# Transposing a normalised row tile one PSUM bank at a time, with every other bank read by VectorE

## The chip, the cores and the metric

One core of a Trainium2 chip runs the whole program. The metric is the device time of one execution in microseconds (us); the kernel before takes 2774.78 us, the median of 3 runs (2773.95 to 2774.79).

## The reference, cut to what matters

One layer of a hybrid decoder is computed for 1024 prompt rows and 64 sample rows (1088 rows of 1024 values, float32). What matters here stands between the mixer and the feed-forward part:

```python
def decoder_layer(x, ...):
    mix, new_win, hg_state = token_mixer(rms_norm(x, norm_mix_pre), ...)   # ends in merged @ w_out
    x = x + rms_norm(mix, norm_mix_post)
    f, conv_buf = conv_ffn(rms_norm(x, norm_ffn_pre), conv_buf0, w_ffn_a, w_ffn_b, ffn_conv_w, ffn_conv_b, w_ffn_d)
    x = x + rms_norm(f, norm_ffn_post)
```

So for each row: the product with `w_out`, a norm, the addition of `x`, a second norm with the gains `norm_ffn_pre`, and then the feed-forward products, which need the normalised rows transposed (features on the partitions).

## The kernel before, in words

The kernel has three phases. Phases 1 and 2 (projections, attention, recurrence, memory attention, gates) are not touched. Phase 3 (`phase3`, from L1386) goes through the 1088 rows in nine row tiles: tiles 0 to 7 of 128 rows, and tile 8 of the 64 sample rows. They are taken in the order 0 and 2 together, then 1, 3, 4, 6, 5, 7, 8. For each tile there are three steps.

- `sums` (L1418): the product with `w_out`, 48 matmuls of 512 columns (8 blocks, 2 halves, 3 products of high and low parts) into two PSUM banks (L1428). The banks come from three pools of two: `ps_u` (tiles 0, 3, 5), `ps_n` (2, 4, 8) and `ps_d` (1, 6, 7). So tile 4 must have read its sums before the matmuls of tile 8 can start.
- `norms` (L1433): `x` is loaded (L1438, on the queue of SyncE, in order), the sums are squared on ScalarE (L1442), the factor is found by `rstd` (L160 to L165, tiny operations that go between VectorE and ScalarE), the sums are scaled (L1447) and `x` is added (L1448) on VectorE, the result is stored by a DMA of GpSimd (L1449), squared on ScalarE (L1451), a second `rstd`, and the rows are scaled on ScalarE (L1453) into `pn_x`. `pn_x` and `pn_y` have two buffers each, so the load of `x` for a tile waits until the transposes of the tile two before it have read their `pn_x`.
- The transposes, at the end of `norms`: eight chunks of 128 x 128 are transposed on TensorE (L1458), four into each of two PSUM banks `ps_t`, and each chunk is copied on ScalarE with its gain (L1461) into `R`. There are only those two `ps_t` banks, and the framework keeps two engines from touching one bank of one tile at the same time: a transpose into a bank waits for the copy of the chunk before it in that bank. With two banks, two transposes can be under way, one for each bank, and then their two copies.

From pairs of tiles, `combos` (L1531) makes on ScalarE and VectorE the sums and splits that the first feed-forward products read: columns 0 to 511 (called t = 0) need tiles 0 to 3, columns 512 to 1087 (t = 1) tiles 4 to 8. `prep_a` with `side_a` (L1565 to L1598) loads and splits the feed-forward weights, in SBUF that held `w_out` (its load, L1578, waits for the last matmul on it). `up` (L1606) does the products, 84 matmuls for each t (L1627). The last three kinds of product of t = 0 need PSUM banks that `ps_n` and `ps_t` held, so they wait for the last copy of the last tile and for the small state that is transposed after it (L1502, copied at L1504). Two blocks of `combos` and the weights are traced under `behind`, which makes the scheduler place them after a given instruction.

Each engine and each DMA queue runs its instructions in an order fixed when the kernel is built, by a list scheduler with a model of the times; at run time an instruction that waits holds up all behind it on its engine.

Of the kernel before, what the change touches and what calls it, by code (L numbers as in the profile page):

```python
# [21 lines left out]
AF = mybir.ActivationFunctionType  # L22
ALU = mybir.AluOpType
AX = mybir.AxisListType

P = 128
# [33 lines left out]
VR_BIN, VR_FFN, VR_HGN, VR_LB = 0, 80, 88, 89  # L60
# [59 lines left out]
class Builder:  # L120
# [1265 lines left out]
    def phase3(self, early):  # L1386

        tc, nc, I, O = self.tc, self.nc, self.I, self.O
        PS = bass.MemoryType.PSUM
        with ExitStack() as es:  # L1390
# [42 lines left out]
            def norms(i, ps, R, half):  # L1433

                a, e = ROWT[i]
                rows = e - a
                x = xp.tile([P, D], F32, name="pn_x")[:rows]
                nc.sync.dma_start(x, self.xrows(a, e))  # L1438
                y = xp.tile([P, D], F32, name="pn_y")[:rows]
                ss = self.sm.tile([P, 2], F32, name="pn_ss")[:rows]  # L1440
                for u in range(2):
                    nc.scalar.activation(y[:, :512], ps[u], AF.Square, accum_out=ss[:, u:u + 1])  # L1442
                nc.vector.tensor_add(ss[:, 0:1], ss[:, 0:1], ss[:, 1:2])
                r = self.rstd(ss[:, 0:1], rows, D)
                for u in range(2):
                    v = slice(u * 512, (u + 1) * 512)
                    nc.vector.scalar_tensor_tensor(y[:, v], ps[u], r, gb[:rows, v], op0=ALU.mult, op1=ALU.mult)  # L1447
                    nc.vector.tensor_add(y[:, v], y[:, v], x[:, v])  # L1448
                nc.gpsimd.dma_start(self.x1d[a:e], y)  # L1449
                s2 = self.sm.tile([P, 1], F32, name="nrm_ss")[:rows]  # L1450
                nc.scalar.activation(x, y, AF.Square, accum_out=s2)  # L1451
                r = self.rstd(s2, rows, D)
                nc.scalar.activation(x, y, AF.Copy, scale=r)  # L1453
                for c in range(8):
                    if c % 4 == 0:
                        pt = self.next_bank()
                    p = pt[:, c % 4 * P:c % 4 * P + rows]
                    nc.tensor.transpose(p, x[:, c * P:(c + 1) * P], self.ident[:rows, :rows])  # L1458
                    g = self.vec[:, VR_FFN + c:VR_FFN + c + 1]
                    dst, src = (R[:, c], p.rearrange("p (h n) -> p h n", h=2)) if half is None else (R[:, c, half], p)  # L1460
                    nc.scalar.activation(dst, src, AF.Copy, scale=g)  # L1461
            new_R = lambda w=P: self.rp.tile([P, 8, 2, w], F32, name=f"R{w}", bufs=2 if w == P else 1)

            tiles = [(i, *sums(i, *b)) for i, b in ((0, (self.pu, "ps_u")), (2, (pnp, "ps_n")))]
# [4 lines left out]
            for j, (i, ps, _) in enumerate(tiles):  # L1469
                norms(i, ps, R02, j)  # L1470
# [3 lines left out]
            for i, pl, nm in order:  # L1474
                ps, step = sums(i, pl, nm)
                steps = [step(k) for k in ((0, 1, 7, 2, 3, 4, 5, 6) if i == 8 else range(8))]
                if i == 3:
                    with self.behind(steps[-1]):
                        self.combos(0, R02, 0, yp[0], "gxy")
                elif i == 8:  # L1480
                    ew.close()
                    self.uw, self.ut, fs = pool(eu, "uw", 1, side="right"), pool(eu, "ut", 2, side="right"), pool(eu, "fs", 1, side="right")
                    self.slots = [(self.wp, "w_hi", 2), (self.wp, "w_hi", 2), (self.wp, "w_lo", 2), (self.wp, "w_lo", 2)] + 3 * [(self.uw, "wx", 3)]
                    self.aside, self.aready = self.side_a(), deque()
                    with self.behind(steps[5]):
                        self.prep_a(7)
                if i in (1, 4, 5):
                    R = new_R()
                elif i == 8:
                    R = new_R(NS // 2)  # L1490
                norms(i, ps, R, None if i == 8 else int(i in (3, 6, 7)))
                if i == 3:
                    self.combos(0, R, P, yp[0], "gxy")
                elif i in (6, 7, 8):
                    late.append((R, {6: 0, 7: P, 8: 2 * P}[i]))
                    if i == 6:
                        self.combos(1, R, 0, None, "g")
# [387 lines left out]
```

## Time and profile before

| | |
|---|---|
| median of 3 runs | 2774.78 us |
| the profiled execution's own time | 2770.02 us |
| its span, first to last instruction | 2767.8 us |
| TensorE busy | 2652.2 us, 96% |
| VectorE busy | 1654.2 us, 60% |
| ScalarE busy | 1096.3 us, 40% |
| mean granted TensorE clock | 0.985 |
| transposes L1458 and copies L1461 | 72 of each, 1575 to 1689 us |

The profile is of one execution. Times within it are counted from the start of its span. Busy time is when an engine executes; waits are put down to the event that released them. A granted clock of 1.00 is 2.4 GHz, of 0.50 is 1.2 GHz; a value between is a mean over a stretch. In a chain of waits a matmul's time is the step to the next one; in a list of instructions it is the longer time from its start to its end, which overlaps the next.

### The profile page before, as it was taken

Reading aid. Unit: us, or ns where it says so; the run is one execution under the profiler, and the core shown is the slowest. Engines: PE = TensorE matmul, PEld = TensorE weight load, DVE = VectorE, ACT = ScalarE, POOL = GpSimd, SP = SyncE. Lnnn points to the kernel's source line nnn. Section 1 sums busy time; section 2 is a strip of 40 time slices with the busy share of each in tenths; the row PEclk is TensorE's granted clock in tenths of the full one; section 3 lists DMA queues with packets and bytes.
Section 4 is the critical chain, followed back from the end, with each engine's and each line's share of the span. In section 5 each row is a group of like instructions: output and inputs, shape, how many; then the busy total and the mean of one; then the engine's idle time right before and its main releaser. Section 6 shows DMA issues by size and latency. Waiting matters only on the chain.

```text
span 2767.8 us, 45536 instructions
## 1 busy us (share of the span) xinstructions
PE 2652.2 (96%) x17822; PEld 2391.7 (86%) x17822; DVE 1654.2 (60%) x3972; ACT 1096.3 (40%) x2036; POOL 196.2 (7%) x339
## 2 busy tenths in 40 slices
PE   7999999999899999999999977999999999999998
PEld 6988888888788989999889856999999999888886
DVE  7246657657556745444447457777777776843536
ACT  5324526435346454444422356333333333411212
POOL 2110010000011000000000000100010001000000
PEclk9999999999999999999999988999999999999999
DMA  7466676867767323222376332333332322531303
GB/s 227 129 181 177 182 223 186 207 190 180 206 190 188 108 94 108 95 92 87 115 245 216 136 121 73 113 119 109 109 100 90 104 77 79 182 113 63 126 32 129
DMA packets 344552, 380.72 MB, mean 138 GB/s; under 512 B 57068, under 2 KB 295076, under 8 KB 343417
## 3 DMA queue, kind: packets, MB, share of 16 engines
q1 hardware_dynamic: 321808, 311.13, 37.4%
q0 software_dynamic: 22240, 65.63, 7.4%
q8 instruction: 140, 2.29, 0.4%
q10 hardware_dynamic: 288, 1.05, 0.1%
q14 instruction: 76, 0.61, 0.1%
HBM read 302.07 MB, written 123.46 MB: 154 GB/s over the span
## 4 chain that ended last, share of the span: by engine, by line
PE 79%; DMA 7%; issue 7%; DVE 3%; ACT 2%; SPq 1%; POOL 0%; DVEq 0%; POOLq 0%; ACTq 0%
PE ps_d L244 30%; PE ps_u L1627 10%; PE ps_c L1627 7%; PE ps_d L1627 7%; PE ps_u L1784 4%; PE ps_d L1784 4%; PE ps_c L1784 4%; DMA qb<-qrow 2%; DMA kt<-kb 1%; PE ps_d L1428 1%; PE ps_u L1428 1%; PE ps_n L1428 1%; PE ps_c L1776 1%; DMA kc<-in_cache_win_kv 1%; DMA comb<-ocomb 1%
## 5 line engine op out<-in xcount | busy, mean ns | idle before, releaser
L244 PE MATMUL ps_d<-act_h,w_hi 128*128 128x512 f32 (+2 forms) x1920 | 649.1, 338 | 7.9 <-DVE proj L832 7.1
L244 PE MATMUL ps_d<-act_l,w_hi 128*128 128x512 f32 (+2 forms) x1920 | 650.1, 339 | 0.0
L244 PE MATMUL ps_d<-act_h,w_lo 128*128 128x512 f32 (+2 forms) x1920 | 646.0, 337 | 0.0
L244 PEld LDWEIGHTS ps_d<-act_h,w_hi 128*128 128x128 f32 x1920 | 367.6, 191 | 36.8 <-DVE proj L832 7.7
L244 PEld LDWEIGHTS ps_d<-act_l,w_hi 128*128 128x128 f32 x1920 | 367.4, 191 | 30.2 <-issue 4.0
L244 PEld LDWEIGHTS ps_d<-act_h,w_lo 128*128 128x128 f32 x1920 | 367.4, 191 | 27.6 <-issue 2.5
L143 ACT ACTIVATE w_hi<-w_raw 128x1024 fp32r<-128x1024 f32 (+1 forms) x156 | 140.5, 902 | 292.3 <-PE ps_d L244 185.7
L144 DVE TENSOR_TENSOR w_lo<-w_raw,w_hi 128x1024 fp32r<-128x1024 f32 (+1 forms) x124 | 138.4, 1118 | 118.6 <-ACT w_hi L143 116.7
L1066 DVE CUSTOM_DVE_ANT_0 qb<-kc,qb 128x128 f32<-128x128 f32 x384 | 89.3, 287 | 100.1 <-DMA qb<-qrow 82.9
L1627 PE MATMUL ps_u<-Yh,w_hi 128*128 128x288 f32 (+1 forms) x512 | 103.9, 292 | 5.6 <-ACT Yh L143 5.6
L1627 PE MATMUL ps_c<-Yh,wx 128*128 128x288 f32 (+1 forms) x512 | 106.9, 290 | 0.0
L1627 PE MATMUL ps_u<-act_h,w_lo 128*128 128x288 f32 (+1 forms) x512 | 104.7, 289 | 0.1
L1627 PE MATMUL ps_d<-act_h,w_hi 128*128 128x288 f32 (+1 forms) x512 | 103.6, 291 | 0.3 <-DVE pn_y L1447 0.3
L1627 PE MATMUL ps_d<-act_h,w_lo 128*128 128x288 f32 (+1 forms) x512 | 101.6, 288 | 1.3 <-ACT uT L1632 1.3
L1627 PE MATMUL ps_u<-Yh,wx 128*128 128x288 f32 (+1 forms) x512 | 102.5, 289 | 0.0
L1627 PE MATMUL ps_c<-act_h,wx 128*128 128x288 f32 (+1 forms) x512 | 101.4, 288 | 0.0
L244 PE MATMUL ps_d<-ohi,w_hi 128*128 128x256 f32 (+2 forms) x288 | 94.4, 329 | 3.1 <-ACT proj L1144 2.0
L244 PE MATMUL ps_d<-olo,w_hi 128*128 128x320 f32 (+2 forms) x288 | 94.6, 328 | 0.0
L244 PE MATMUL ps_d<-ohi,w_lo 128*128 128x320 f32 (+2 forms) x288 | 94.1, 327 | 0.0
L1144 ACT ACTIVATE proj<-ps_d,nbin 128x512 f32<-128x512 f32 (+2 forms) x96 | 53.2, 554 | 95.0 <-PE ps_d L244 95.0
L143 ACT ACTIVATE wx<-S 128x512 fp32r<-128x512 f32 x64 | 40.5, 632 | 126.3 <-PE ps_c L1627 124.9
L1627 PEld LDWEIGHTS ps_u<-Yh,w_hi 128*128 128x128 f32 x512 | 83.8, 192 | 5.9 <-ACT Yh L143 5.9
(638 smaller groups left out, 6319.2 us busy)
## 6 DMA issues: line engine op xcount, KB each, us to landing
w_raw<-in_w_in SPq DMA_DIRECT2D x80, 512.0 KB, 4.0
out_s_win<-in_cache_win_kv SPq DMA_DIRECT2D x40, 1016.0 KB, 7.2
kc<-in_cache_win_kv SPq DMA_DIRECT2D x80, 256.0 KB, 3.9
qb<-qrow SPq DMA_DIRECT2D x64, 256.0 KB, 4.8
kc<-in_cache_win_kv SPq DMA_DIRECT2D x128, 128.0 KB, 3.6
w_raw<-in_w_ffn_a SPq DMA_DIRECT2D x32, 512.0 KB, 3.7
w_raw<-in_w_ffn_b SPq DMA_DIRECT2D x32, 512.0 KB, 3.6
yd<-ext POOLq DMA_DIRECT2D x32, 512.0 KB, 4.8
```

Source lines behind the costliest of these rows:

```text
L143: self.nc.scalar.activation(hi, src, AF.Copy)
L144: self.nc.vector.tensor_sub(lo, src, hi.bitcast(F32))
L244: nc.tensor.matmul(ps, W[:, c], X(c), start=n == 0, stop=n == 3 * kb - 1)
L1066: nc.vector.tensor_tensor_reduce(q[:, j], k[:, j], q[:, j], 1.0, 0.0, ALU.mult, ALU.add, T[:, c:c + 1])
L1144: self.proj(col, lambda ps, a, e: nc.scalar.activation(y[:, a:e], ps, AF.Exp, bias=nb, scale=-1.0))
L1428: mm = nc.tensor.matmul(ps[u], mg[x][:, k, o:o + e - a], wk[k][w][:, u * 512:(u + 1) * 512], start=k == m == 0, stop=k == (6 if i == 8 els ...
L1627: nc.tensor.matmul(p, w[:, c], self.side_b(t, b, x, c), start=new and m == 0, stop=m == 11, skip_group_check=not new)
L1776: nc.tensor.matmul(self.smp[u], ys, w[x][:, u * 512:(u + 1) * 512], start=first and k + x == 0, stop=last and k + x == G)
L1784: nc.tensor.matmul(ps, y[a][:, i * P:(i + 1) * P], w[b][:, u * 512:(u + 1) * 512], start=m == 0, stop=m == 3 * G - 1)
```

## The change

The eight chunks are taken in two groups of four. All four transposes of a group are traced first, into one bank, and then the bank is copied: the first bank by four copies on ScalarE as before, the second by one multiplication on VectorE, 128 partitions x (4 chunks x rows), with the four gains spread over the rows by a broadcast operand.

```diff
-                for c in range(8):
-                    if c % 4 == 0:
-                        pt = self.next_bank()
-                    p = pt[:, c % 4 * P:c % 4 * P + rows]
-                    nc.tensor.transpose(p, x[:, c * P:(c + 1) * P], self.ident[:rows, :rows])
-                    g = self.vec[:, VR_FFN + c:VR_FFN + c + 1]
-                    dst, src = (R[:, c], p.rearrange("p (h n) -> p h n", h=2)) if half is None else (R[:, c, half], p)
-                    nc.scalar.activation(dst, src, AF.Copy, scale=g)
+                for c in range(0, 8, 4):
+                    pt = self.next_bank().rearrange("p (c n) -> p c n", c=4)[:, :, :rows]
+                    for j in range(4):
+                        nc.tensor.transpose(pt[:, j], x[:, (c + j) * P:(c + j + 1) * P], self.ident[:rows, :rows])
+                    dst = R[:, c:c + 4].rearrange("p c h n -> p c (h n)") if half is None else R[:, c:c + 4, half]
+                    g = self.vec[:, VR_FFN + c:VR_FFN + c + 4]
+                    if c:
+                        nc.vector.tensor_tensor(dst, pt, g.unsqueeze(2).to_broadcast([P, 4, rows]), op=ALU.mult)
+                    else:
+                        for j in range(4):
+                            nc.scalar.activation(dst[:, j], pt[:, j], AF.Copy, scale=g[:, j:j + 1])
```

The arithmetic is the same: each transposed value times its gain.

## Rows read from the trace of the kernel before

**Rows 1.** Windows: stretch, length, busy PE, PEld, DVE, ACT, POOL, granted clock, DMA share, GB/s.
```profile
1562.00:1612.00 50.00, 50.00 (x225) 40.31 (x225) 14.45 (x49) 18.88 (x55) 1.60 (x3) 1.00 0.12 42
1612.00:1622.00 10.00, 3.42 (x15) 1.83 (x14) 9.66 (x20) 8.86 (x21) 0.53 (x1) 0.82 0.47 157
1622.00:1646.00 24.00, 24.00 (x103) 16.69 (x102) 6.23 (x19) 9.50 (x26) 0.53 (x1) 0.93 0.20 67
1646.00:1662.00 16.00, 2.96 (x12) 1.34 (x10) 15.35 (x31) 10.83 (x25) 0.53 (x1) 0.60 0.77 261
1662.00:1677.60 15.60, 11.54 (x66) 9.30 (x66) 12.35 (x34) 13.36 (x41) 1.06 (x2) 0.87 0.29 102
1677.60:1690.00 12.40, 6.23 (x32) 4.55 (x32) 4.21 (x10) 8.87 (x26) 0.54 (x1) 0.73 0.26 63
1690.00:1702.00 12.00, 6.38 (x38) 6.14 (x37) 10.87 (x18) 6.22 (x10) 0.00 (x0) 0.78 0.34 130
1702.00:1712.00 10.00, 10.00 (x60) 9.91 (x61) 4.30 (x14) 2.28 (x6) 0.34 (x1) 0.74 0.01 2
1712.00:2768.00 1056.00, 1041.48 (x6895) 968.71 (x6893) 686.19 (x1345) 331.69 (x545) 61.45 (x133) 1.00 0.32 102
```

**Rows 2.** Waits of TensorE's matmuls, 1712 to 2768 us: all there are.
```profile
PE ps_d L1784 <- DVE yl L144: 1.9, 1, 1.9
PE ps_d L1784 <- ACT yh L143: 1.3, 1, 1.3
```

**Rows 3.** Chain that ended last, 1580 to 1593 us: start, length, engine, tile, line, count.
```profile
1581.64 0.22 PE ps_t L1458 x2
1581.86 4.91 PE ps_n L1428 x21
1586.77 0.22 PE ps_t L1458 x2
```

**Rows 4.** Timeline of ScalarE and VectorE: start, duration, then [idle before, released by].
```profile
1560.43 0.60 ACT L1442 ACTIVATE pn_y<-ps_u 128x512 f32<-128x512 f32 x1 [8.00 <-PE ps_u L1428]
...
1565.32 1.28 DVE L1448 TENSOR_TENSOR pn_y<-pn_y,pn_x 128x512 f32<-128x512 f32 x2
...
1569.12 1.15 ACT L1453 ACTIVATE pn_x<-pn_y,rs_r 128x1024 f32<-128x1024 f32 x1 [0.59 <-DVE rs_r L165]
...
1575.84 0.63 ACT L1461 ACTIVATE R<-ps_t,vec 128x128 f32<-128x128 f32 x2 [0.31 <-PE ps_t L1458]
...
1591.98 0.62 ACT L1461 ACTIVATE R<-ps_t,vec 128x128 f32<-128x128 f32 x2 [4.43 <-PE ps_t L1458]
...
1688.67 0.52 ACT L1461 ACTIVATE R<-ps_t,vec 128x64 f32<-128x64 f32 x2 [0.25 <-PE ps_t L1458]
```

**Rows 5.** Waits of SyncE's queue, 1540 to 1720 us: total, times, longest.
```profile
SPq L1438 <- PE ps_t L1458: 87.9, 7, 39.3
SPq L1578 <- PE ps_d L1428: 25.3, 1, 25.3
```

**Rows 6.** The loads of `x`, line L1438: issue to landing.
```profile
DMA to landing us min/median/max: 3.4/3.6/7.5
```

**Rows 7.** Timeline of TensorE: tile 8's stall, and the last matmul of the sums.
```profile
1612.79 0.38 PE L1458 MATMUL ps_t<-ident,pn_x 128*128 128x128 f32 x2
...
1614.86 0.59 PE L1458 MATMUL ps_t<-ident,pn_x 128*128 128x128 f32 x2 [0.45 <-ACT R L1461]
...
1621.50 0.69 PE L1428 MATMUL ps_n<-w_hi,act_h 128*64 128x512 f32 x1 [5.27 <-DVE pn_y L1447]
...
1646.08 0.39 PE L1428 MATMUL ps_n<-w_row,act_h 128*64 128x512 f32 x1
```

**Rows 8.** Groups by line and shape, 1560 to 1710 us; the last from its line's own view.
```profile
L1461 ACT ACTIVATE R<-ps_t,vec 128x128 f32<-128x128 f32 x64 | 20.6, 362 | 34.5 <-PE ps_t L1458 34.3
L1447 DVE SCALAR_TENSOR_TENSOR pn_y<-ps_d,rs_r,gb 128x512 f32<-128x512 f32 x6 | 4.2, 747 | 0.1
L1504 DVE COPY stT<-ps_t x1: 683/683/683, 1690.6 to 1690.6; 128x512 f32<-128x512 f32 x1
```

## The prediction

> **What bounds the kernel now.** I first read the windows, to see where TensorE, busy for 96% of the span, is not busy. From 1712 us to the end it works 1041.5 of 1056 us at a granted clock of 1.00 [rows 1], and the list of its waits there holds 3.2 us in all [rows 2]. So the rest of the kernel runs at TensorE's pace, and what starts earlier at 1712 ends earlier by as much. Before 1612 it is full too. Between 1612 and 1712 it is not: the idle time of the windows is 6.6 + 13.0 + 4.1 + 6.2 + 5.6 = 35.5 us. In the same windows the clock was granted below 1.00; busy time times what is missing of the clock gives 0.6 + 1.7 + 1.2 + 1.5 + 1.7 + 1.4 + 2.6 = 10.7 us [rows 1]. A window's mean clock also covers its idle part, so I count 9 us of that. The ceiling of any change to this stage is therefore 35.5 + 9 = 44.5 us.
>
> Next I read the chain and the timeline before the idle part, to see what was late. The chain shows a pair of transposes (0.22 us), 21 matmuls of the next sums (4.91 us), and again a pair [rows 3]: each trip from TensorE to ScalarE and back costs a place in TensorE's order, one pair every 5.13 us. The first tile's rows are scaled at 1569.12 + 1.15 = 1570.27, its first copies start at 1575.84 and its last pair ends at 1591.98 + 0.62 = 1592.6: 22.3 us for eight small transposes [rows 4]. The copies waited 34.3 us for transposes [rows 8]; meanwhile ScalarE is busy 18.9 of 50 us and VectorE 14.5 [rows 1]. Nobody is short of time there; the trips are the limit.
>
> Then the waits of SyncE's queue show how this reaches the sums: the loads of `x` waited 87.9 us, seven times, for transposes that had to free `pn_x` [rows 5]. With its `x` late, tile 4 freed its `ps_n` banks late, and tile 8's sums stood still: after 1612.79 TensorE did eight transposes and nothing else until 1621.50, the last 5.27 us of it waiting for L1447 [rows 7]. The norms of the last tiles then fall behind the end of the sums.
>
> **The change, part by part.** It removes 36 of 72 ScalarE copies, at 0.63 / 2 = 0.31 us each in a pair [rows 4], 11 us of an engine that is not the limit. It removes three of four trips per tile. It adds nine multiplications on VectorE. The trace has none with a broadcast operand; the nearest rows for 128x512 out of PSUM are a plain copy, 0.683 us, and a two-operand one, 0.747 us [rows 8]. I take 0.72, with both as bounds: 6.5 us of VectorE in all. The transposes are the same 72. No DMA is added; the nine loads of `x` on SyncE and the stores of the result on GpSimd move earlier, and with them the weight loads queued behind on SyncE. The added wait is VectorE's, for the fourth transpose of the second bank; behind it on VectorE stand the next tile's `rstd`, L1447 and L1448, and the weight work of `prep_a`.
>
> *One tile after, with TensorE full.* One placement behind 21 matmuls (4.9 us), eight transposes at 0.11 us (0.9), then four ScalarE copies (1.2) beside one multiplication (0.72): 7 us from the scaled rows instead of 22.3, so 15 us less. The loop of one `pn_x` buffer is then: load 3.6 us [rows 6], from L1448 to the end of L1453 1570.27 - 1565.32 = 4.95 us [rows 4], placement 4.9, transposes 0.9, together 14.4 us. Two buffers turn, so a tile can pass every 7.2 us. The sums of a tile take 48 x 4.91 / 21 = 11.2 us [rows 3]. The norms keep up with the sums, where today they don't.
>
> *Step 1, the sums.* Tile 8's stall goes: 1621.50 - 1612.79 = 8.7 us [rows 7]; tile 4's banks are read some 20 us before they are wanted. The clock of the stretch after it, 0.93 for 24 us [rows 1], gives back 1.7. Against it, transposes of later tiles move ahead of the end of the sums: 56 (seven tiles) instead of the 24 that lie outside the stall today, 32 x 0.11 = 3.5 us. The sums end at 1646.3 [rows 7] - 8.7 - 1.7 + 3.5 = 1639.4.
>
> *Step 2, from the end of the sums to the last copy.* Today that is 1688.67 + 0.52 = 1689.2 [rows 4], 42.9 us after the sums, for the norms of tiles 6, 5, 7, 8 and most of tile 4's transposes. After the change only tiles 7 and 8 are left. Tile 8 by itself takes 1570.27 - 1560.43 = 9.8 us from squaring to scaled rows [rows 4], 0.9 for transposes and 1.2 for copies: 1651.4. It shares VectorE with `prep_a` and `combos`, which today keep it busy 15.35 of 16 us [rows 1]; I put half of that in its way, 7.7 us, since about half of the norms in that stretch will be done. The last copy then ends at 1659.1, 30.1 us earlier.
>
> *Step 3, from there to full speed.* From 1689.2 to 1712 VectorE works nearly all of the first 12 us (10.87) on splits and sums of t = 1 that are placed behind the last copy, then TensorE catches up [rows 1]. The change touches none of it: 22.8 us stay, and this is the wait that is late next.
>
> The sum is 30 us. Against the profiled execution's own 2770.0 us that makes 2740. It ran 4.8 us under the median of 2774.8, so I carry the difference over: **2744.8 us**.
>
> Copying in one piece has a price too: a bank's first copy starts only after its fourth transpose, 3 x 0.11 = 0.33 us later than now, 3 us over nine tiles if all were on the path. I count it inside the eight transposes. The Trainium skill, Perfetto Trace Analysis, section Optimizing Tensor Performance, advises that independent groups rotate through PSUM banks so that emptying one overlaps the next; today's order does rotate, and by that rule the change would lose those 3 us and win nothing. The row speaks for more: with TensorE idle a trip still takes (1614.86 - 1612.79) / 2 = 1.03 us [rows 7], so the four of today cost 4.1 us where the new order needs about 2.
>
> **The rivals.** *The end is held by VectorE and the weights.* The weight loads wait for the last use of `w_out` (25.3 us, [rows 5]), and VectorE has 15.35 + 12.35 + 4.21 + 10.87 = 42.8 us of work in the 56 us to 1702 [rows 1], in order. If only the sums get shorter (6.9 us) and of that work only the sums' scaling and additions of two tiles move out (4 x 0.75 + 4 x 0.7, 6 us), the gain is 13 us: 2762. For it speaks the dense stretch from 1646 to 1662; against it, that VectorE idles 8 of 12.4 us just before 1690.
>
> *Slower: VectorE's order becomes the path.* If the last five tiles (4, 6, 5, 7, 8) are limited by VectorE and not by trips, each multiplication adds its 0.72 us and blocks the queue for one trip, 1.03 us, while the transposes that it waits for come: 5 x 1.75 = 8.8 us, 2783.6. It decides from the point at which the loads of `x` no longer wait for transposes; the 87.9 us of such waits [rows 5] speak against it, the full VectorE after 1646 for it. The Trainium skill, Perfetto Trace Analysis, section Optimizing Scalar/DVE Operations, says that where these engines aren't saturated but cause bubbles elsewhere, breaking instructions up may let work finish sooner; the change does the opposite. The windows agree with the rule's condition (18.9 and 14.5 of 50 us); no row here shows its result.
>
> *The change doesn't do what it says.* If the scheduler still places something between transposes of one bank, the trips' delay stays as TensorE's order and little moves: 2774. Nothing but the order of the build excludes it; matmuls that share a bank do follow each other undisturbed now, the 21 of the chain among them [rows 3].
>
> **How the numbers follow.** The forecast has a chance of 0.62; its own range is a gain of 18 to 40 us (all of the dense 15.35 us in tile 8's way with a little more, or none of it with some clock back), 2735 to 2757. VectorE and the weights: 0.22. Nearly the whole ceiling (over 40 us): 0.03. No effect: 0.06. Slower: 0.07. Two parts in a thousand, 5.5 us, is about what a measurement can tell here; so faster is 0.62 + 0.22 + 0.03 = 0.87, same 0.06, slower 0.07. The multiplication's bounds move the sum by under 0.4 us. The range runs from nearly the ceiling (2732) to past the first rival (2766) and leaves out the last two cases.
>
> **What would show it.** In the changed profile: eight transposes of a tile in a row, one wait for L1453 and none for L1461 between them; the nine multiplications near 0.72 us; the loads of `x` waiting for transposes far less than 87.9 us; no wait of tile 8's first matmul for L1447; the sums ending near 1639, the last copy near 1659 and full speed from about 1682. Wrong would be a last copy after 1675 with VectorE full before it (the first rival), VectorE waiting for L1458 with norms queued behind it (the second), or transposes still apart (the third).

## The result, and the profile after

The changed kernel took 2741.78 us, the median of four runs (2738.69 to 2744.65), beside 2774.73 us for the kernel before (2773.95 to 2774.79): a ratio of 0.9882, 95% interval 0.9865 to 0.9899. The profiled execution took 2738.69 us, with a span of 2736.8 us and a mean granted clock of 0.989.

Not all of the 31.0 us between the two profiled spans (2767.8 and 2736.8) belongs to the change. A stage has to be measured from its own start, and the first square of tile 0 (ScalarE, L1442) starts at 1560.43 us before [rows 4] and at 1554.70 after, 5.7 us earlier, though the program up to there is the same. From here on I use three numbers for each profile: the **stage** (from that square to the end of the last copy into `R`), the **rest** (from there to the end of the span), and their sum. Before: 128.8, 1078.6 and 1207.4 us. After: 101.7, 1080.4 and 1182.1 us. So the change won 27.1 us in the stage, gave 1.8 back behind it, and is worth 25.3 us in this profile.

The windows of the changed kernel, cut at the end of the sums (1633.5), the last copy (1656.4) and full speed (1679.2); columns as in [rows 1]:

```profile
1555.00:1612.00 57.00, 57.00 (x269) 46.52 (x268) 38.36 (x99) 36.04 (x97) 3.19 (x6) 1.00 0.26 93
1612.00:1622.00 10.00, 10.00 (x49) 8.21 (x48) 6.88 (x18) 5.41 (x13) 0.53 (x1) 1.00 0.41 145
1622.00:1633.50 11.50, 11.50 (x56) 7.25 (x55) 6.20 (x16) 5.00 (x15) 0.53 (x1) 1.00 0.62 165
1633.50:1645.00 11.50, 6.89 (x43) 6.41 (x43) 9.93 (x17) 10.04 (x22) 0.00 (x0) 0.85 0.62 218
1645.00:1656.40 11.40, 5.33 (x37) 4.48 (x36) 7.11 (x19) 3.63 (x10) 0.54 (x1) 0.79 0.23 63
1656.40:1669.20 12.80, 8.13 (x40) 7.27 (x40) 10.25 (x14) 6.04 (x10) 0.00 (x0) 0.77 0.32 121
1669.20:1679.20 10.00, 8.49 (x48) 8.40 (x49) 4.78 (x16) 2.73 (x7) 0.00 (x0) 0.68 0.01 2
1679.20:2736.80 1057.60, 1043.07 (x6907) 969.92 (x6905) 686.65 (x1347) 332.64 (x546) 61.84 (x133) 1.00 0.32 102
```

The window 1612 to 1622, which held tile 8's stall in [rows 1] (3.42 of 10 us busy), is now full at a clock of 1.00, as is everything up to the end of the sums. Before, ScalarE and VectorE were busy 18.9 and 14.5 of 50 us there; now the norms' work lies beside the sums, at 36 and 38 of 57 us. The idle rest is 4.61 + 6.07 + 4.67 + 1.51 = 16.9 us between 1633.5 and 1679.2. In the last window TensorE leaves 14.53 us free, as it did before (1056.00 - 1041.48, [rows 1]).

The chain of the changed kernel (start, length, engine, tile, line, count) answers to [rows 3]; the timeline of ScalarE and VectorE answers to [rows 4]:

```profile
1569.96 0.87 PE ps_t L1457 x8
1570.84 2.07 PE ps_u L1428 x9
1572.90 3.89 PE ps_n L1428 x17
1576.79 0.87 PE ps_t L1457 x8
```

```profile
1554.70 0.60 ACT L1442 ACTIVATE pn_y<-ps_u 128x512 f32<-128x512 f32 x1 [8.01 <-PE ps_u L1428]
...
1563.39 1.15 ACT L1453 ACTIVATE pn_x<-pn_y,rs_r 128x1024 f32<-128x1024 f32 x1 [0.58 <-DVE rs_r L165]
...
1570.44 1.14 ACT L1464 ACTIVATE R<-ps_t,vec 128x128 f32<-128x128 f32 x4 [0.64 <-PE ps_t L1457]
1570.87 0.69 DVE L1461 TENSOR_TENSOR R<-ps_t,vec 128x512 f32<-128x512 f32 x1 [0.70 <-PE ps_t L1457]
...
1655.48 0.93 ACT L1464 ACTIVATE R<-ps_t,vec 128x64 f32<-128x64 f32 x4 [0.78 <-PE ps_t L1457]
```

A tile's eight transposes stand in one row of 0.87 us, and the four copies of one bank run beside the multiplication of the other. Tile 0's rows are scaled at 1564.54 and its copies end at 1571.58: 7.0 us, where it took 22.3.

### The profile page after: what moved, and what is told of

The parts are those of the page before. It is cut to its first block, busy times and chain, and to the rows that moved or that the text cites. A ratio compares the mean times of both kernels' runs of the same rounds, so it can differ in the third digit from the quotient of the medians.

```text
span 2736.8 us, 45512 instructions
## 1 busy us (share of the span) xinstructions
PE 2640.7 (96%) x17822; PEld 2387.3 (87%) x17822; DVE 1659.2 (61%) x3981; ACT 1085.8 (40%) x2000; POOL 196.8 (7%) x339
## 4 chain that ended last, share of the span: by engine, by line
PE 82%; DMA 6%; issue 6%; DVE 3%; ACT 2%; SPq 1%; POOL 0%; DVEq 0%; POOLq 0%; ACTq 0%
PE ps_d L244 32%; PE ps_u L1630 10%; PE ps_c L1630 7%; PE ps_d L1630 7%; PE ps_u L1787 4%; PE ps_d L1787 4%; PE ps_c L1787 4%; DMA qb<-qrow 2%; PE ps_d L1428 1%; PE ps_u L1428 1%; DMA kt<-kb 1%; PE ps_c L1779 1%; PE ps_n L1428 1%; PE ps_sc L1226 1%; DMA qrow<-qn 1%
## 5 line engine op out<-in xcount | busy, mean ns | idle before, releaser
L1630 PE MATMUL ps_u<-Yh,wx 128*128 128x288 f32 (+1 forms) x512 | 103.0, 290 | 2.5 <-DVE u L1643 2.5
L1630 PE MATMUL ps_c<-act_h,wx 128*128 128x288 f32 (+1 forms) x512 | 101.4, 288 | 0.0
L244 PE MATMUL ps_d<-olo,w_hi 128*128 128x320 f32 (+2 forms) x288 | 95.2, 331 | 0.0
```

Source lines behind the costliest of these rows:

```text
L244: nc.tensor.matmul(ps, W[:, c], X(c), start=n == 0, stop=n == 3 * kb - 1)
L1630: nc.tensor.matmul(p, w[:, c], self.side_b(t, b, x, c), start=new and m == 0, stop=m == 11, skip_group_check=not new)
```

## The experiments

Four kernels went beside each other first: the changed one again, and three that share the copies out in another way.

**The changed kernel again.**

> The changed kernel once more, beside the others. The stage, from the first squaring of tile 0 (L1442) to the last copy into R, took 101.7 us after the change and 128.8 us before it, 27.1 us less; the profiled execution was 31 us shorter, since it reached the stage 5.7 us earlier in an order of work that is the same up to there. If those 5.7 us are chance of single executions, this run comes again between 2738 and 2746 us and the start of the stage moves by a few us from run to run; if the change itself made them, the stage starts near 1555 us again.

Measured: 2746.38 us (2742.85 to 2753.09), ratio 0.9915 (0.99 to 0.9929). Its stage is 101.1 us and the sum 1181.7, within 0.6 us of the first profile; but the stage starts at 1561.52 us instead of 1554.70. The time that differs between the two profiles lies before the stage; the median came out just above the expected 2738 to 2746.

**Both banks on ScalarE.**

```diff
-                    if c:
+                    if False:
```

> Four transposes a bank as in the change, but both banks copied on ScalarE, no multiplication on VectorE. Theory (the trips between TensorE and the copying engine decide): within 4 us of the changed kernel, stage 98 to 106 us. Rival 1 (the relief of ScalarE is what pays): a third or more of the gain is lost, over 2752 us, stage over 110 us. Rival 2 (VectorE's order is the path, the nine multiplications cost): 4 to 9 us faster than the changed kernel, stage 93 to 98 us.

Measured: 2745.58 us, ratio 0.9905 (0.989 to 0.992). Stage 101.1 us, sum 1180.8.

**Both banks on VectorE.**

```diff
-                    if c:
+                    if True:
```

> Both banks copied by one multiplication on VectorE each, nothing on ScalarE: nine more multiplications of 0.68 us on VectorE and 36 copies fewer on ScalarE. Theory (trips decide, the engine hardly): within 4 us of the changed kernel. Rival 1 (relief of ScalarE pays): 4 us or more faster than the changed kernel. Rival 2 (VectorE's order is the path): 4 to 9 us slower than the changed kernel, stage 105 to 110 us.

Measured: 2743.46 us, ratio 0.9901 (0.9889 to 0.9914). Stage 100.9 us, sum 1179.4.

**The old order, half of its copies on VectorE.**

```diff
-                    nc.scalar.activation(dst, src, AF.Copy, scale=g)
+                    if c < 4:
+                        nc.scalar.activation(dst, src, AF.Copy, scale=g)
+                    else:
+                        nc.vector.tensor_scalar(dst, src, g, None, op0=ALU.mult)
```

> The kernel before, one transpose and one copy at a time in each bank, but the second bank's copies on VectorE, one 128x128 multiplication by the gain each. Four trips a tile as before. Theory (trips decide): no gain, 2770 to 2778 us, stage 125 to 132 us. Rival 1 (sharing the copies between two engines pays): half of the gain or more, under 2760 us, stage under 116 us.

Measured: 2778.87 us, ratio 1.0028 (1.0017 to 1.004). Stage 135.0 us, sum 1214.2. Two rows of the chain and one of VectorE's waits (total, times, longest) in this kernel:

```profile
1586.19 0.22 PE ps_t L1458 x2
...
1591.23 0.22 PE ps_t L1458 x2
```

```profile
DVE R L1464 <- PE ps_t L1458: 40.6, 19, 4.9
```

The pairs are 5.04 us apart (5.13 in [rows 3]). There is no gain, as the theory has it, but the stage and the time came out above its 125 to 132 and 2770 to 2778 us. With the old order, help from VectorE costs 6.2 us of stage: its copies wait 40.6 us for transposes, and what is queued behind them on VectorE waits too. That this wait makes the 6.2 us is read from the trace, not tried by itself. With whole banks it makes no difference to the stage which engine copies: 101.1, 100.9 and 101.1 to 101.7 us. What the change is worth comes from the transposes' order; the multiplication on VectorE, the other half of it, adds nothing that shows. (With both banks on VectorE the rest behind the stage was 1078.5 us, 2 us under the changed kernel's; that is one profile, and the ratios overlap.)

**Two trips a tile.** Two transposes and their two copies, then the bank's other two, ScalarE alone:

```diff
-                    for j in range(4):
-                        nc.tensor.transpose(pt[:, j], x[:, (c + j) * P:(c + j + 1) * P], self.ident[:rows, :rows])
...
+                    for k in range(0, 4, 2):
+                        for j in range(k, k + 2):
+                            nc.tensor.transpose(pt[:, j], x[:, (c + j) * P:(c + j + 1) * P], self.ident[:rows, :rows])
+                        for j in range(k, k + 2):
+                            nc.scalar.activation(dst[:, j], pt[:, j], AF.Copy, scale=g[:, j:j + 1])
```

> Two transposes of a bank are traced, then their two ScalarE copies, then the bank's other two: a tile's eight transposes take two trips from TensorE to the copies and back, where the kernel before takes four and the changed one takes one; ScalarE does all copies, as before. If it is the number of trips that costs the time, the stage (first square of tile 0 to last copy into R; 128.8 us before, 101 to 102 us in every kernel with whole banks so far) lands between them, at 104 to 114 us, and the ratio to the kernel before is 0.991 to 0.997. Rival: what counts is only whether a wait for a copy stands between a bank's transposes at all; then the stage stays within 4 us of 128.8 us and the ratio is 0.998 to 1.002. Second rival: four transposes in a row are already enough to hide the trips; then the stage is within 2 us of 101.5 us and the ratio is that of the changed kernel, about 0.990.

Measured: 2750.99 us, ratio 0.9926 (0.991 to 0.9942). Stage 106.0 us, sum 1184.5. Four transposes stand together, and the next four where they find a place: 25 matmuls on, as two pairs with one matmul between them, and then again 20 on (chain):

```profile
1573.61 0.44 PE ps_t L1460 x4
1574.04 2.08 PE ps_u L1428 x9
1576.13 3.66 PE ps_n L1428 x16
1579.79 0.22 PE ps_t L1460 x2
1580.01 0.24 PE ps_n L1428
1580.25 0.22 PE ps_t L1460 x2
1580.47 4.66 PE ps_n L1428 x20
1585.13 0.22 PE ps_t L1460 x2
```

The stage lies between one trip (101.1 to 101.7) and four (128.8), nearer to one: the second trip costs 4 to 5 us, the third and fourth 23 together. With two trips the sums end 77.5 us into the stage, no later than with one (78.8), so what the second trip costs lies behind the sums, in the norms of the last tiles. With four they end at 85.9 ([rows 7], [rows 4]): there the norms fall behind the sums too, and more of them are left over for the end. That this alone makes the 23 us is the theory's reading of the three points, not a separate measurement.

**VectorE's multiplication twice.**

```diff
-                        nc.vector.tensor_tensor(dst, pt, g.unsqueeze(2).to_broadcast([P, 4, rows]), op=ALU.mult)
+                        for _ in range(2):
+                            nc.vector.tensor_tensor(dst, pt, g.unsqueeze(2).to_broadcast([P, 4, rows]), op=ALU.mult)
```

> The changed kernel with each of VectorE's nine multiplications made twice, with the same values: 6 us more work on VectorE (9 x 0.68 us), inside the stretch in which it was feared to become the bound. If VectorE is not on the path but for the last tiles, the stage grows by the second multiplications of tiles 7 and 8 alone, 0 to 1.4 us, and the ratio to the kernel before is within 0.002 of the changed kernel's (about 0.990). If VectorE's order of work is the path (the rival by which the change would have been slower), every copy delays the splits behind it, the stage grows by 4 to 7 us, and the ratio is 0.993 or more.

Measured: 2745.19 us, ratio 0.9908 (0.9892 to 0.9924). Stage 102.0 us, sum 1181.3. The view of the tile `R` holds all 18 (line, engine, operation, count: ns min/median/max):

```profile
L1462 DVE TENSOR_TENSOR R<-ps_t,vec x18: 424/684/692, 1572.9 to 1658.3; 128x512 f32<-128x512 f32 x16, 128x256 f32<-128x256 f32 x2
```

Six microseconds more on VectorE add 0.2 to 0.8 us to the stage. VectorE is not the bound while the sums run.

**What holds tile 8's norm.** In the changed kernel tile 8's squares end at 1639.47 us and its first residual product (L1447) starts at 1648.14, 8.7 us later; for tile 7 it is 1.5 us. Work on VectorE and ScalarE that prepares the next stage stands between. Five versions move it. The first leaves three of the seven weight preparations behind the sixth block of tile 8's sums (`steps[5]`), where all seven were, and puts four behind tile 8's residual sums:

```diff
-                    nc.vector.tensor_add(y[:, v], y[:, v], x[:, v])
+                    self.added = nc.vector.tensor_add(y[:, v], y[:, v], x[:, v])
...
                     with self.behind(steps[5]):
-                        self.prep_a(7)
+                        self.prep_a(3)
...
                 norms(i, ps, R, None if i == 8 else int(i in (3, 6, 7)))
+                if i == 8:
+                    with self.behind(steps[5]), tc.issue_after(self.added.ins):
+                        self.prep_a(4)
```

> The changed kernel, with four of the seven weight preparations that are put off into the end of the stage issued behind the residual sums of tile 8, so that VectorE comes to tile 8's norm before them. If these splits on VectorE delay tile 8's norm by 7 to 8 us, as the prediction has it, the last copy into R comes 4 to 8 us earlier after the stage's start (94 to 98 us in place of 101.5), and the time falls by 3 to 7 us against the changed kernel (ratio to the kernel before about 0.988) unless the moved splits are then waited for by TensorE after the stage, which gives the same time as the changed kernel with an earlier last copy. Rival: tile 8's norm is held by the sums and ScalarE alone; then the last copy stays within 1 us of 101.5 us.

Measured: 2748.85 us, ratio 0.9921 (0.9903 to 0.9939). Stage 103.0 us, sum 1184.6: neither theory's number. VectorE's timeline shows why:

```profile
1642.50 1.40 DVE L1447 SCALAR_TENSOR_TENSOR pn_y<-ps_n,rs_r,gb 64x512 f32<-64x512 f32 x2
...
1648.88 0.14 DVE L164 TENSOR_SCALAR rs_u<-rs_u 64x1 f32<-64x1 f32 x1
1649.95 0.69 DVE L1590 TENSOR_TENSOR S<-w_raw 128x512 f32<-128x512 f32 x1 [0.94 <-DMA w_raw<-in_w_ffn_b]
1650.56 0.14 DVE L165 TENSOR_TENSOR rs_r<-rs_r,rs_u 64x1 f32<-64x1 f32 x1
```

L1447 comes 1.5 us earlier in the stage (91.9 instead of 93.4), but the moved work now cuts the second half of the norm in two: the last step of its `rstd` (L165) stands behind a sum that waits 0.94 us for a weight's DMA. The work had moved, but not past the norm.

The second and third put it behind tile 8's scaled rows (L1453), all seven preparations or four (the second is shown). Their loads are not held back by this edit:

```diff
-                nc.scalar.activation(x, y, AF.Copy, scale=r)
+                self.scaled = nc.scalar.activation(x, y, AF.Copy, scale=r)
...
-                    with self.behind(steps[5]):
-                        self.prep_a(7)
...
+                if i == 8:
+                    with self.behind(self.scaled):
+                        self.prep_a(7)
```

> The changed kernel, with the copies and splits of all seven put-off weight preparations issued behind the scaled rows of tile 8 instead of behind tile 8's sums; their loads stay early. In the changed kernel tile 8's squares are done 8.7 us ahead of its first residual product, where tile 7's take 1.5 us, because other work stands between on VectorE; of that the splits of tile 7's rows (four, 3.6 us) stay. If VectorE's queue is what holds tile 8's norm, the last copy into R comes at 95 to 98 us of the stage, in place of 101.5 us. If the sums, ScalarE or the transposes hold it, it stays within 1 us of 101.5 us. The time of the whole is another matter: TensorE's products that ran ahead of the last copy in the changed kernel now have no weights until after it, so the time is that of the changed kernel or up to 12 us more (ratio to the kernel before 0.990 to 0.995): whoever holds that the last copy alone sets the end expects 4 to 6 us less (0.988).

> The same with three preparations where the changed kernel has them and only the other four behind tile 8's scaled rows. In the version that put the four behind the residual sums, tile 8's first residual product came 1.5 us earlier in the stage, and the moved splits then took 2.5 us back in the second half of the norm. If it is the place in VectorE's queue, the last copy now comes 1 to 3 us earlier than the changed kernel's 101.5 us (98 to 100.5 us), and the time is within 4 us of the changed kernel's, either way (ratio to the kernel before 0.988 to 0.992), as what is put off is wanted by TensorE soon after. If the splits had nothing to do with it, the last copy stays at 101 to 103 us.

Measured, all seven: 2742.81 us, ratio 0.9889 (0.9867 to 0.9912); stage 95.2, rest 1082.8, sum 1178.1 us. Four: 2743.42 us, ratio 0.9898 (0.9873 to 0.9923); stage 99.3, rest 1081.7, sum 1181.1 us. Both last copies came where VectorE's place in the queue was expected to put them, 6 and 2 us earlier. With all seven behind, 2.4 us of the 6 are given back after the last copy, so the whole came out under the 0.990 to 0.995 that was expected of it. Of the loads only the first three stayed early: the fourth is issued 93.2 us into the stage, where the changed kernel has it at 82.5.

The fourth also puts the splits of tile 7's rows behind, and the fifth does the same but leaves three preparations early; the changed kernel ran beside them:

```diff
-            with self.behind(steps[-1]):
+            with self.behind(self.scaled):
                 for R, o in late:
                     self.combos(1, R, o, None, "x")
```

> As with all seven preparations behind tile 8's scaled rows, and the splits of tile 7's rows behind them too, so that nothing of VectorE's stands between tile 8's squares and its scaled rows. If the 3.6 us of these splits were the rest of the wait, the last copy into R comes another 3 to 4 us earlier, at 91 to 93 us of the stage (101.5 in the changed kernel, 95.2 with the preparations behind). What was put off is then wanted sooner after the last copy than it is ready: from the last copy to the end 1083 to 1087 us instead of 1080.5, so that from the stage's start to the end it is 1175 to 1179 us (changed kernel 1182). If the put-off work is the bound of the next stretch, the whole of the 3 to 4 us is given back (1178 to 1181 us).

> As the last, but three of the preparations stay where the changed kernel has them, for TensorE to have products ahead of the last copy; four preparations and the splits of tile 7's rows stand behind tile 8's scaled rows. Last copy at 92 to 96 us of the stage; from the last copy to the end less than with all seven behind, 1080 to 1084 us; from the stage's start to the end 1174 to 1179 us. If early weights are worth nothing, it comes out no better than the version with all behind.

> The changed kernel unaltered, beside the two versions above on one chip: last copy at 101 to 102 us of the stage, 1180 to 1183 us from the stage's start to the end, ratio to the kernel before 0.988 to 0.992. If the versions are truly faster, theirs are 0.001 to 0.003 lower.

Measured, all behind: 2743.34 us, ratio 0.99 (0.9886 to 0.9914); stage 94.3, rest 1083.0, sum 1177.4 us. Three early: 2748.41 us, ratio 0.9925 (0.9907 to 0.9944); stage 98.7, rest 1083.7, sum 1182.4. The changed kernel: 2746.53 us, ratio 0.9917 (0.9905 to 0.993); stage 101.4, rest 1080.4, sum 1181.8. The stage of 94.3 us missed the 91 to 93 expected. Three early missed its 92 to 96 and its sum of 1174 to 1179 us, and its rest is no shorter than with all behind, so preparations left early were worth nothing. Its rows are scaled 14.5 us after the end of the sums; 2.9 of these pass before tile 8's first square, which stands behind tile 7's scaling; that is late after ScalarE's wait of 1.83 us for the load of a weight that was left early (more on this wait under step 2). ScalarE's timeline with all behind:

```profile
1650.98 1.15 ACT L1453 ACTIVATE pn_x<-pn_y,rs_r 64x1024 f32<-64x1024 f32 x1 [0.64 <-DVE rs_r L165]
1652.04 0.62 ACT L143 ACTIVATE w_hi<-w_raw 128x512 fp32r<-128x512 f32 x1
1652.56 0.61 ACT L143 ACTIVATE w_lo<-w_raw 128x512 fp32r<-128x512 f32 x1
1653.08 3.03 ACT L143 ACTIVATE act_h<-R 128x512 fp32r<-128x512 f32 x4
...
1657.58 0.89 ACT L1464 ACTIVATE R<-ps_t,vec 128x64 f32<-128x64 f32 x4
```

From the end of the sums to the scaled rows it is now 9.2 us (1642.97 to 1652.13), about the 9.8 us of a tile by itself: nothing that shows stands in the norm's way any more. But nine put-off copies run on ScalarE ahead of the last four into `R`, which end 6.3 us after the scaled rows instead of 1.7. What is moved out of one queue's way was put into another's.

By the profiles the versions with all seven preparations behind are about 4 us faster than the changed kernel (sums 1177.4 and 1178.1 against 1181.7 to 1182.1). Their ratios, 0.9889 and 0.99, lie below its 0.9915 and 0.9917, but the intervals overlap: the runs don't establish it.

## Why the prediction was right

The direction, the size and the mechanism came out as forecast: 30 us were expected and 25 are shown by the profiles' sums. The changed kernel's median went from 2741.8 us in the first comparison to 2746.4 and 2746.5 in the later two, all near the 2744.8 forecast; but the ratios there, 0.9915 and 0.9917, are 23 to 24 us, so the first comparison's 33 us is not to be taken for the change's own worth. That the first median lies only 3 us from the forecast has luck in it: in the profiles the change fell 5 us short of the 30, and the stage happened to start 5.7 us earlier.

*What bounds the kernel.* Right. From full speed on both profiles leave the same 14.5 us idle, and the time followed the last copy to within 1.8 us. The later versions show a limit to this: a last copy 6 us earlier gained about 4 by the profiles' sums.

*The trips.* Right, and shown: the three ways to copy with whole banks agree within 0.8 us of stage, and two trips lie between one and four. The time from tile 0's scaled rows to its last copy is 7.0 us as forecast. The Trainium skill, Perfetto Trace Analysis, section Optimizing Scalar/DVE Operations, says that where these engines aren't saturated but cause bubbles elsewhere, breaking instructions up may let work complete sooner. These runs show no gain from it: with one 0.68 us multiplication for each bank the stage was as long as with four copies (100.9 against 101.1 us). The single copies on VectorE in the old order (135.0 us) don't test it, since they have four trips a tile as well.

*Each term of the change.* The multiplication measured 0.684 us (forecast 0.72, bounds 0.683 to 0.747), by its row in the view of `R`:

```profile
L1461 DVE TENSOR_TENSOR R<-ps_t,vec x9: 424/684/692, 1570.9 to 1655.9; 128x512 f32<-128x512 f32 x8, 128x256 f32<-128x256 f32 x1
```

Copying in one piece cost nothing that shows: tile 0's 7.0 us are the sum that was forecast with it. The prediction read the rotation of banks as speaking for the order before; but the changed order fills its two banks in turn as well, and empties them side by side (ScalarE from 1570.44, VectorE from 1570.87), so this doesn't tell the two orders apart.

*Step 1, the sums.* Forecast to end 79.0 us into the stage (1639.4 - 1560.43); they end at 78.8 (1633.53 - 1554.70), and at 78.8 again in both repeats. The stall is gone, and 56 transposes stand ahead of the end of the sums, as the prediction counted.

But the link that the prediction drew from trips to stall was half of it. It said that the loads of `x` come late because they wait for transposes, and that tile 4's banks were freed late for want of its `x`. But L1447, which frees them, doesn't read `x`; what it waited for stood ahead of it on VectorE. It also expected those waits to shrink to far less than 87.9 us. They are still there, with no stall behind them (SyncE's queue after, total, times, longest):

```profile
SPq L1438 <- PE ps_t L1457: 71.0, 7, 23.8
```

So this total alone doesn't tell whether a wait costs time; one that does is shown under step 2. The timeline of VectorE in the kernel before shows a second link (rows not shown ahead):

```profile
1611.65 0.69 DVE L1547 TENSOR_TENSOR G<-R 128x512 f32<-128x512 f32 x1 [9.14 <-ACT R L1461]
...
1616.01 1.29 DVE L1448 TENSOR_TENSOR pn_y<-pn_y,pn_x 128x512 f32<-128x512 f32 x2
...
1619.00 0.14 DVE L160 TENSOR_SCALAR rs_v<-pn_ss 128x1 f32<-128x1 f32 x1
...
1620.70 1.41 DVE L1447 SCALAR_TENSOR_TENSOR pn_y<-ps_n,rs_r,gb 128x512 f32<-128x512 f32 x2
```

VectorE waited 9.14 us with a sum of `G` for the last copies into `R`. Behind it in its queue stood tile 3's residual sums (L1448) and tile 4's `rstd` (L160), though tile 4's squares had been done since 1602.3. Tile 3's load of `x` was issued at 1612.05 and takes 3.5 us, so it came at 1615.6, 0.4 us before VectorE got there. Both links hang on the same trips, and the term is right by either; that the loads alone would have made the stall was not shown, nor tried.

*Step 2, from the sums to the last copy.* Forecast 19.7 us (1639.4 to 1659.1), measured 22.9 (1633.53 to 1656.41). This is the mis-sized term: other work in tile 8's way was put at 7.7 us. From the sums' end to the scaled rows (1654.71) it took 21.2 us where a tile alone takes 9.8, so 11.3 us stood in the way; transposes and copies then took 1.7 instead of 2.1. The prediction counted VectorE alone. ScalarE's queue delays the norm too, and ahead of that stands the load of a weight (the chain of the changed kernel):

```profile
1625.69 0.89 PE ps_t L1457 x8
...
1626.63 0.51 SPq L1438
...
1627.23 6.48 DMA w_raw<-in_w_ffn_a
...
1633.73 0.64 ACT w_lo L143
...
1634.40 0.69 DVE w_lo L144
1635.09 0.08 DVE rs_r L165
...
1635.22 1.03 issue
1636.25 0.67 ACT pn_y L1442 x2
1636.92 1.99 ACT act_h L143 x3
1638.90 0.57 ACT pn_y L1442 x2
```

In SyncE's queue the load of tile 8's `x` (L1438) waited for a tile's transposes, and the load of a weight stood behind it. ScalarE waited 1.67 us for that weight, VectorE's split of it came after, and behind the split stood the last step of tile 7's `rstd` (L165), though the step before it had ended at 1632.51. So tile 8's first square starts 2.7 us after the sums' end, behind tile 7's late scaling, and its second stands behind 2.0 us of splits. The wait for the weight is in all three profiles of the changed kernel (1.36 to 1.67 us) and in the three versions that leave three preparations early (1.83 to 2.15), and not in the two with all seven behind. By itself it is not the bound: with both banks on VectorE tile 8's first square starts 0.1 us after the sums' end, and its rows are still scaled 20.5 us after it. That VectorE and ScalarE's order holds this norm is shown: with that work behind the scaled rows, the 11.3 us fell to 3.2 (1640.16 to 1653.15, less 9.8) and then to nothing. How the 11.3 us divide among the preparations' splits and sums, the splits of tile 7's rows and the weight's load is not shown.

*Step 3, from the last copy to full speed.* Forecast 22.8 us unchanged. The cut at 1679.2 lies the same 22.8 us behind the last copy, but the work is not as far there: 12 matmuls more are left than at 1712 before (6907 against 6895), and the rest is 1.8 us longer. TensorE's first matmul on the last split of t = 1 starts 14.3 us after the last copy; before, it started 12.7 us after (timeline of TensorE, before and after):

```profile
1701.91 0.61 PE L1627 MATMUL ps_u<-Yh,w_hi 128*128 128x288 f32 x1 [5.62 <-ACT Yh L143]
```

```profile
1670.71 0.61 PE L1630 MATMUL ps_u<-Yh,w_hi 128*128 128x288 f32 x1 [5.62 <-ACT Yh L143]
```

The last split on VectorE ends 14.8 us after the last copy; before, it ended 13.3 us after. So what was late next was named rightly, and its 5.6 us wait is as long as before. What makes the 1.6 us was not tried; in the chain after, 12 matmuls on `ps_c` (2.6 us) stand ahead of 11 on `ps_d`, which came first before.

*The rivals.* That VectorE and the weights hold the end with a gain of 13 us: not so, the last copy came at 1656.4. Its mechanism shows, though, in the 11.3 us of step 2 and in the later versions: what they put behind the scaled rows costs 1.3 to 3.3 us after the last copy (rest 1081.7 to 1083.7 against 1080.4). That VectorE's order becomes the path and the kernel slower: with the changed order, doubling the multiplication added at most 0.8 us. With the old order it happened, by 6.2 us of stage, so its price of 8.8 came near and its condition was wrong: it wants several trips a tile that VectorE must wait for. That the change does nothing: eight transposes stand in a row.

## What to carry to other kernels

A transpose that is copied before the next one is traced makes a round trip between two queues for each, and each trip waits for a place in the busy engine's order (here 21 matmuls, 5.1 us, on); trace all that a bank holds, and then empty it, with whichever engine is free. Read what a head of a queue waits for together with what stands behind it: here one sum's 9.14 us wait on VectorE kept a finished norm waiting, and a weight's late load held up a norm that didn't need it. Measure a stage from its own start, since here the start alone moved by 20 us from profile to profile.

## What the runs showed that was not expected

The start of the stage, at the end of more than 1500 us of work that is the same in all these kernels, ranges from 1550.6 to 1570.7 us over 14 profiles, while the stage repeats within 0.6 us (101.1 to 101.7) in the three profiles of the changed kernel. TensorE was busy 941.5 of the first 1000 us at a granted clock of 0.99 in the earliest, 933.6 at 0.98 in the latest. So most of the spread between these profiles comes from there, and what makes it stays open. It is as large as most changes that one would try on this stage; the stage's own length tells apart what the medians don't.
